# Query projections of five heads by seven products, output projections spread over the heads, and the softmax ratio on GpSimd

## The chip, the core and the metric

The kernel runs on one core of a Trainium2 chip, in one launch. The metric is the device time of that launch in microseconds (us), the median of the timed runs. Names used throughout: TensorE (PE) does matrix products, VectorE (DVE) elementwise work, ScalarE (ACT) activations and copies, GpSimd (POOL) small vector work, SyncE (SP) issues most of the DMAs.

## The reference, cut to what matters

A trunk of two layers over 16 meta tokens and 512 real ones, model width 1024, in float32: a gated linear attention layer first, then a differential attention layer with eight heads of two 128-wide maps. The change touches the second layer alone:

```python
proj = xn @ w_in                              # 1024 -> 8192
q, k, v, z = jnp.split(proj, 4, axis=-1)      # per head: q, k two maps of 128, v and z 256 wide
s = einsum(q, k) * scale + bias;  s = where(dist >= 0, s, -inf)
p = softmax(s);  a = p[:, :, 0] - lam * p[:, :, 1]
o = einsum(a, vh)
o = head_rms(o) * gnorm * (1.0 - lambda_init)
y = silu(z) * o;  h = h + y @ w_out;  out = rmsnorm(h[:, N_META:], g_final)
```

## The kernel before, in words

**Precision.** A float32 operand is split into a high part (a copy in the fast float32 format, by ACT) and a low part (source minus high part, by DVE), and a product is three passes: high by high, high by low, low by high. `split` (lines 269 to 280) does this for tokens, queries, keys and weights, so each 128x1024 piece of weights costs one ACT and one DVE instruction; its pieces are called wh and wl.

**Plain and seven-product projections.** A head needs four projections (q, k, v, z), each a 1024 by 256 piece of the weights. The plain form, `project` (line 421), takes each half of 128 output columns through 24 matmuls of 512 tokens, 48 in all. The other form, `Unit` (line 431), cuts weights and tokens into two by two blocks and forms the result by seven block products instead of eight (the scheme of Strassen and Winograd): seven products of 12 matmuls, 84 in all, each 256 or 264 tokens wide. It wants sums of token blocks (t1 to t4, made once for the layer by `token_sums2`), and for each piece of weights four additions of 128x512 blocks (line 366), three single blocks to be split (a11, a12, a22) and two pairs of blocks (s21, s43). Out of its products it makes three partial copies (u, line 452) and four additions into the result (lines 477 to 481). Before the change z, v and k of heads 1 to 7 are made by units and q of all heads by the plain form (`q_diff_q`).

**Order of the work.** PE runs in the order in which the program is written; DVE, ACT and POOL run in an order that a scheduler makes out of priorities (`urgent`, `soon`, `at_once`). A `Weaver` holds a queue of generators (projections and output projections). While head hd does its attention, `W.fill` puts pieces of that queue between the 16 attention steps: A (scores, lines 1675 to 1688), B (`turn`, transposes of the weights of attention, lines 1695 and 1696), C (`values`, lines 1400 and 1711, with the norm at 1715 to 1719) and E (`rows`, lines 1725 and 1728), over four blocks of 128 query rows, largest first. The matmuls of the scores and the values stand in a helper at line 400. The queue of a head holds z, v, k and q of the next head; the next head begins when its q is finished. In head 6, q of head 7 comes before v and z.

**Output projections.** `q_diff_out2` takes the finished rows y of two heads (two pairs of 512 output columns) and adds their product to the accumulator `hacc` (line 1771). It stands ahead of z in the queue of heads 2, 4 and 6, for the pairs (0,1), (2,3), (4,5); those of 6 and 7 are done at the end (`final_rows`).

**Homes.** The rows y of a head lie in one of two places (`yt`, by `hd % 2`). The values of a head lie in a pool with two buffers (`v_tiles`). Values leave the projection transposed, go to DRAM and come back by transposing DMAs of SP (`turn_by_dma`); `place`, `done` and `rest` then copy and split them into the value tiles, 0.0 or 11.0 us of woven work later, for odd and even heads.

**The ratio.** Behind the two exponentials of a block (line 1682), DVE takes the reciprocal of the second map's sum (line 1685), multiplies it by lambda and by the first map's sum (1686), and subtracts the maps in one instruction (1687).

**Weights.** `Weights` loads for the first two jobs of its list and prepares their pieces as soon as a buffer is free (two pairs, one of a11, a12, a22 and the sums).

## Time and profile before

| | us |
|---|---|
| timed runs (3): median, lowest, highest | 972.43, 972.37, 973.35 |
| profiled execution: span from first to last instruction | 970.2 |
| PE busy in it | 957.1 (99%) |
| DVE, ACT, POOL busy | 778.4 (80%), 628.0 (65%), 50.6 (5%) |
| heads 0 to 7 begin at (first row of each head's own woven work) | 496, 549, 601, 675, 728, 802, 854, 909 |

The page gives no total time of the profiled execution beside its span; the median of the timed runs is 2.2 us (0.23%) above the span. Busy time of PE counts a matmul from its start to a modelled end, so one matmul's busy time is longer than the step from it to the next: where a step is meant, starts are subtracted. A group's line has the source line, engine, operation and tiles, then the count, the busy time in us and the mean in ns, then the idle time of the engine ahead of it and what ended it.

### The profile page before, as it was taken

What the parts mean: (1) busy time and instruction counts of PE and PEld (TensorE: products, weight loads), DVE (VectorE), ACT (ScalarE), POOL (GpSimd) and SP (SyncE); (2) the same over time, 40 slices, a digit from 0 to 9 for tenths busy, and PEclk for the clock granted to TensorE, in tenths of its full rate; (3) what the DMA queues carried; (4) which work ended last, traced back from release to release, by engine and by line L of the source; (5) the groups of instructions that cost most, each with busy time, mean ns of one, the idle gap of its engine ahead of it and who ended that gap; (6) DMA issues with size and microseconds to landing.
All of it is one profiled execution on the core that took longest, in us unless ns stands there. A gap on an engine that the chain in (4) does not pass through costs nothing. (4 is left out here: it accounts for less than half of the span.)

```text
span 970.2 us, 18065 instructions
## 1 busy us (share of the span) xinstructions
PE 957.1 (99%) x6993; PEld 906.5 (93%) x6993; DVE 778.4 (80%) x1586; ACT 628.0 (65%) x1304; POOL 50.6 (5%) x68
## 2 busy tenths in 40 slices
PE   8999999999999999999999999999999999999997
PEld 8999999999999999898899998898998999989996
DVE  7989885886888887568997985977958879677785
ACT  7776755577647567656757774576764677655583
POOL 1000000000000100000001001001010000000001
PEclk9999999999999999999999999999999999999999
DMA  7322223635363245224355525135252352412212
GB/s 197 88 86 60 79 81 122 148 99 129 120 156 96 79 121 154 62 92 151 100 132 147 131 78 153 51 97 140 86 148 88 99 138 86 148 61 84 87 66 87
DMA packets 128521, 104.94 MB, mean 108 GB/s; under 512 B 51101, under 2 KB 112829, under 8 KB 128432
## 3 DMA queue, kind: packets, MB, share of 16 engines
q1 hardware_dynamic: 123104, 93.80, 35.1%
q10 hardware_dynamic: 5328, 9.95, 2.8%
q8 instruction: 56, 0.92, 0.4%
q14 instruction: 33, 0.27, 0.1%
HBM read 83.64 MB, written 11.80 MB: 98 GB/s over the span
## 5 line engine op out<-in xcount | busy, mean ns | idle before, releaser
L277 DVE TENSOR_TENSOR wl<-raw,wh 128x1024 fp32r<-128x1024 f32 x98 | 119.5, 1222 | 24.8 <-ACT wh L276 16.8
L276 ACT ACTIVATE wh<-raw 128x1024 fp32r<-128x1024 f32 x98 | 103.2, 1055 | 52.6 <-PE by L968 23.2
L431 PE MATMUL bv<-x,wh 128*128 128x264 f32 (+1 forms) x656 | 97.6, 286 | 0.0
L431 PE MATMUL bx<-x,wh 128*128 128x264 f32 (+1 forms) x640 | 94.9, 286 | 0.7 <-ACT u L452 0.6
L431 PEld LDWEIGHTS bv<-x,wh 128*128 128x128 f32 x656 | 86.5, 188 | 0.6 <-DVE z L479 0.3
L431 PEld LDWEIGHTS bx<-x,wh 128*128 128x128 f32 x640 | 84.5, 188 | 1.9 <-ACT u L452 1.2
L452 ACT ACTIVATE u<-bx 128x264 f32<-128x264 f32 (+1 forms) x120 | 45.4, 380 | 32.3 <-PE bx L431 31.1
L421 PE MATMUL bx<-x,wh 128*128 128x512 f32 (+1 forms) x256 | 62.4, 386 | 0.0
L277 DVE TENSOR_TENSOR wl<-sum,wh 128x1024 fp32r<-128x1024 f32 x41 | 50.1, 1221 | 14.3 <-ACT wh L276 13.9
L431 PE MATMUL bv<-x,wl 128*128 128x264 f32 (+1 forms) x328 | 55.2, 285 | 0.1
L1718 POOL TENSOR_TENSOR st<-st,mhalf 128x1 f32<-128x1 f32 x32 | 31.0, 970 | 464.4 <-ACT on L1716 408.9
L431 PE MATMUL bx<-x,wl 128*128 128x264 f32 (+1 forms) x320 | 53.9, 285 | 0.0
L1682 ACT ACTIVATE p<-p,st 128x528 f32<-128x528 f32 (+3 forms) x64 | 36.5, 571 | 25.4 <-DVE st L1680 24.9
L421 PEld LDWEIGHTS bx<-x,wh 128*128 128x128 f32 x256 | 44.5, 188 | 7.9
L276 ACT ACTIVATE wh<-sum 128x1024 fp32r<-128x1024 f32 x41 | 43.3, 1056 | 13.0 <-PE bv L431 4.0
L431 PE MATMUL by<-x,a12h 128*128 128x264 f32 (+1 forms) x320 | 46.5, 285 | 0.2 <-ACT t L1646 0.2
L431 PE MATMUL bx<-x,a11h 128*128 128x264 f32 (+1 forms) x320 | 46.3, 285 | 0.0
L431 PEld LDWEIGHTS bv<-x,wl 128*128 128x128 f32 x328 | 45.9, 188 | 0.4 <-issue 0.3
L431 PEld LDWEIGHTS bx<-x,wl 128*128 128x128 f32 x320 | 45.2, 188 | 0.6 <-DVE wl L277 0.2
L276 ACT ACTIVATE a11h<-raw 128x512 fp32r<-128x512 f32 x41 | 25.7, 627 | 28.6 <-DMA raw<-in_diff_w_in_dram 14.2
L431 PEld LDWEIGHTS bx<-x,a11h 128*128 128x128 f32 x320 | 42.2, 188 | 0.7
L431 PEld LDWEIGHTS by<-x,a12h 128*128 128x128 f32 x320 | 41.8, 188 | 0.4 <-ACT t L1646 0.4
(475 smaller groups left out, 2632.2 us busy)
## 6 DMA issues: line engine op xcount, KB each, us to landing
raw<-in_gla_w_in_dram SPq DMA_DIRECT2D x48, 512.0 KB, 4.5
raw<-in_diff_w_in_dram SPq DMA_DIRECT2D x42, 512.0 KB, 4.8
raw<-in_diff_w_in_dram SPq DMA_DIRECT2D x11, 1024.0 KB, 6.3
raw<-in_gla_w_out_dram SPq DMA_DIRECT2D x8, 1024.0 KB, 5.7
raw<-in_diff_w_out_dram SPq DMA_DIRECT2D x8, 1024.0 KB, 6.4
vd<-planes ACTq DMA_DIRECT2D x12, 268.0 KB, 7.1
vd<-keep ACTq DMA_DIRECT2D x12, 264.0 KB, 2.3
T<-bdr SPq DMA_DIRECT2D x8, 264.0 KB, 5.0
```

The lines of the kernel that those rows point to most:

```text
L276: act.activation(hi, src, AF.Copy)
L277: dve.tensor_tensor(lo, src, hi.bitcast(F32), op=ALU.subtract)
L421: pe.matmul(bank, a[:, k, :], b[k] if n0 is None else b[k][:, n0 + i * nn:n0 + (i + 1) * nn], start=n == 0 and ks[0] == 0, stop=n == len(t ...
L431: pe.matmul(bank[:, :x[q].shape[2]], w[p][:, k * P:(k + 1) * P], x[q][:, k, :], start=first and i == 0, stop=i == len(PASSES) - 1, skip_gr ...
L452: W.moved = act.activation(t, self.bx[:, :self.n], AF.Copy, scale=self.sc)
L1682: act.activation(p[:, :nk], p[:, :nk], AF.Exp, scale=-1.0, bias=st[:, m:m + 1], accum_out=st[:, 2 + m:3 + m])
L1718: pool.tensor_tensor(ms, ms, mhalf[:, :1], op=ALU.pow)
```

## The change

Four things are changed together; PE's order is the same up to head 2 of the second layer; heads 0 and 1 are touched only by the ratio and by when the values are placed.

1. **Queries of heads 3 to 7** go through a `Unit` (84 matmuls of 256 tokens) in place of the plain form (48 of 512). The unit's result lands in two float32 tiles and is split from there (`tail`).
2. **Output projections** are woven a half at a time: columns 0 to 511 of a pair in the even head, the rest in the odd head behind it; the last pair (4,5) keeps both halves in head 6. So that the rows of a pair live one head longer, rows get a third home, `y3`, and go by `hd % 3`.
3. **Values** have one home in place of two: they are placed only once their head has begun (`ready`, `begun`), 1.0 us of woven work after that. The last head's values take over `y3`.
4. **The ratio** goes to GpSimd in three instructions (power, times lambda, product); DVE keeps the subtraction of the maps.

```diff
     def turn_by_dma(planes, groups, ends, us, done, last, direct=False, ready=None):
...
-            W.follow((us, place), (1.5, lambda: done(raw[:, :, :P], tick[0], 0)), (2.5, lambda: done(raw[:, :, P:], tick[0], 1)),
+            steps = ((us, place), (1.5, lambda: done(raw[:, :, :P], tick[0], 0)), (2.5, lambda: done(raw[:, :, P:], tick[0], 1)),
                      (1.5, rest))
+            if ready is None:
+                W.follow(*steps)
+            else:
+                ready(steps)
...
     def v_tiles(s):
-        s.v = [T(ep, [P, 4, 256], F32R, f"v{i}") for i in range(2)]
+        if s is heads[-1]:
+            t = T(ep, [P, 2, 2, NR], F32R, "y3", bufs=1)
+            s.v = [t[:, j].rearrange("p a (b c) -> p (a b) c", c=256) for j in range(2)]
+        else:
+            s.v = [T(ep, [P, 4, 256], F32R, f"v{i}", bufs=1) for i in range(2)]
...
-                                      [(slice(3, 1, -1), 0), (slice(1, None, -1), 272)], 240, 0.0 if heads.index(s) % 2 else 11.0, done, last)
+                                      [(slice(3, 1, -1), 0), (slice(1, None, -1), 272)], 240, 1.0, done, last, ready=lambda steps: W.follow(*steps) if s.begun else ready.append(steps))
...
     def q_diff_q(hd, s):
+        scale, qts = -float(P) ** -0.5, []
+
+        def tiles():
+            assert not hd or heads[hd - 1].scored
+            s.q = [T(ep, [P, 2, NR], F32R, f"q{j}", bufs=1) for j in range(2)]
+
+        if hd in (3, 4, 5, 6, 7):
+            def dst():
+                tiles()
+                qts.extend([tok_tile()[:, :NR], tok_tile()[:, :NR]])
+                return qts
+
+            @soon
+            def tail(i):
+                split(*[t[:, i, :] for t in s.q], qts[i])
+
+            return W.add(Unit(want_unit(d_w_in, 256 * hd), Xr, scale, dst, tail), 8.9)
         want_diff(256 * hd)
...
-            dve.reciprocal(st[:, 5:6], st[:, 3:4])
-            dve.scalar_tensor_tensor(st[:, 5:6], st[:, 5:6], lam, st[:, 2:3], op0=ALU.mult, op1=ALU.mult)
+            pool.tensor_tensor(st[:, 5:6], st[:, 3:4], minus, op=ALU.pow)
+            pool.tensor_tensor(st[:, 4:5], st[:, 2:3], lam, op=ALU.mult)
+            pool.tensor_tensor(st[:, 5:6], st[:, 5:6], st[:, 4:5], op=ALU.mult)
             dve.scalar_tensor_tensor(r.p[0], r.p[1], st[:, 5:6], r.p[0], op0=ALU.mult, op1=ALU.subtract)
...
-    def q_diff_out2(hd, yp):
+    def q_diff_out2(hd, yp, halves):
...
-            for i in range(2):
+            for i in halves:
...
-        return W.add(gen(), 22.4)
+        return W.add(gen(), 11.2 * len(halves))
...
+    yt = [yt[:, 0], yt[:, 1], T(ep, [P, 2, 2, NR], F32R, "y3", bufs=1)]
...
         W.finish(projs[hd])
         W.settle()
-        s.scored = False
+        for chain in ready:
+            W.follow(*chain)
+        ready.clear()
+        s.scored, s.begun = False, True
...
-        if hd in (2, 4, 6):
-            out2 = q_diff_out2(hd - 2, ys[hd - 2:hd])
+        if 2 <= hd < D_HEADS - 1:
+            pair = hd - 2 - hd % 2
+            out2 = q_diff_out2(pair, ys[pair:pair + 2], range(2) if hd == D_HEADS - 2 else [hd % 2])
...
-                ys.append([yt[:, hd % 2, i] for i in range(2)])
+                ys.append([yt[hd % 3][:, i] for i in range(2)])
```

**PE at the end of a query projection.** The first rows are of the kernel before, where the queries of head 4 end (bx is the bank they gather in, x the tokens, wh and wl the weights) and the output projection of heads 0 to 3 begins (hT holds the rows y).

```order
L421 MATMUL bx_11926<-x_1514_8556,wh_11859 128x512
L421 MATMUL bx_11926<-x_1515_8557,wh_11859 128x512
L421 MATMUL bx_11926<-x_1512_8554,wl_11860 128x512 x4
L421 MATMUL bx_11926<-x_1514_8556,wl_11860 128x512 x4
L400 MATMUL bx_11960<-wh_11972,hT_8779 128x512
L400 MATMUL bx_11960<-wl_11973,hT_8779 128x512
L400 MATMUL bx_11960<-wh_11972,hT_8779 128x512 x2
```

The same place now: the last two of the seven products, 256 tokens wide, with the second half of the output projection of heads 2 and 3 behind them (y is the third home).

```order
L431 MATMUL by_12067<-x_1514_8558,a12l_11908 128x256 x4
L431 MATMUL bx_12081<-x_1544_8789,a22h_12005 128x256 x8
L431 MATMUL bx_12081<-x_1544_8789,a22l_12006 128x256 x4
L431 MATMUL bv_12028<-x_1514_8558,wh_12001 128x256
...
L431 MATMUL bv_12028<-x_1514_8558,wl_12002 128x256 x4
L400 MATMUL bx_12112<-wh_12125,y_1540_8782 128x512
L400 MATMUL bx_12112<-wl_12126,y_1540_8782 128x512
L400 MATMUL bx_12112<-wh_12125,y_1540_8782 128x512 x2
```

The first scores of a head that begins with an output projection stand, in both kernels, 18 matmuls of 512 columns behind the last query matmul. Before, that was so in heads 2, 4 and 6; now it is so in heads 2 to 6.

**DVE at the start of head 4.** Before: the low parts of the queries (line 280, the second one read straight out of PSUM) and the first scores (line 1680).

```order
L280 SCALAR_TENSOR_TENSOR q_2136_11923<-bx_11868,q_2135_11922 128x512
L1728 TENSOR_TENSOR yt_11942<-ps_11939,z_10814 128x256
L277 TENSOR_TENSOR hT_8779<-yt_11942,hT_8779 128x2x128
L277 TENSOR_TENSOR wl_11977<-raw_11964,wh_11976 128x1024
L280 SCALAR_TENSOR_TENSOR q_2136_11923<-bx_11926,q_2135_11922 128x512
L1680 ISA p_12002,st_12001<-ps_12003,T_11698 128x264
```

Now, from the addition that ends the unit (line 481) to the first scores (line 1710); `tick` opens the placing of the head's values.

```order
L481 SCALAR_TENSOR_TENSOR t_12064<-bv_12028,u_12026 128x256
L366 TENSOR_TENSOR raw_12122<-raw_12122 128x4x128
L277 TENSOR_TENSOR wl_12130<-raw_12116,wh_12129 128x1024
L277 TENSOR_TENSOR q_2161_12063<-t_12065,q_2160_12062 128x512
L277 TENSOR_TENSOR q_2161_12063<-t_12064,q_2160_12062 128x512
L616 MEMSET tick_12150 128x1
L366 TENSOR_TENSOR raw_12122<-raw_12122,sum_12140 128x4x128
L277 TENSOR_TENSOR a22l_12270<-raw_12122,a22h_12269 128x512
L1710 ISA p_12170,st_12169<-ps_12171,T_11708 128x264
```

Both halves of the queries' low parts now stand behind the unit's last addition, and so behind PE's last query matmul.

**The ratio of the first block of head 4.** Before, on DVE, from the last of the scores to the subtraction of the maps (line 1687):

```order
L1680 ISA st_12001 128x1
L366 TENSOR_TENSOR sum_12098<-raw_11980 128x512
L277 TENSOR_TENSOR a12l_12157<-raw_11980,a12h_12156 128x512
L366 TENSOR_TENSOR sum_12098<-sum_12098,raw_11980 128x512
L1685 RECIPROCAL st_12001<-st_12001 128x1
L1771 TENSOR_TENSOR keep_8187<-keep_8187,bx_11960 128x512
L1686 SCALAR_TENSOR_TENSOR st_12001<-st_12001,lam 128x1
L277 TENSOR_TENSOR wl_12036<-raw_11970,wh_12035 128x1024
L1687 SCALAR_TENSOR_TENSOR p_12002<-p_12014,st_12001,p_12002 128x528
```

Now, on DVE, over the same stretch:

```order
L1710 ISA st_12169 128x1
L412 SCALAR_TENSOR_TENSOR vm_12160<-lands_12120,short,vm_12160 32x256
L277 TENSOR_TENSOR wl_12207<-sum_12140,wh_12206 128x1024
L1718 SCALAR_TENSOR_TENSOR p_12170<-p_12182,st_12169,p_12170 128x528
L1802 TENSOR_TENSOR keep_8189<-keep_8189,bx_12112 128x512
```

Five other instructions of DVE stood between scores and subtraction, and now two; the ratio's two instructions are gone from DVE, and the subtraction there waits for GpSimd.

More of the change, by code (lines that the diff above doesn't have):

```diff
@@ L576, in landed, with turn_by_dma @@
         dve.tensor_tensor(lo, src, hi.bitcast(F32), op=ALU.subtract)
-    def turn_by_dma(planes, groups, ends, us, done, last, direct=False):
+    def turn_by_dma(planes, groups, ends, us, done, last, direct=False, ready=None):
         n = planes.shape[2]
@@ L621, in trunk @@
     dve.memset(mhalf, -0.5)
+    minus = cp.tile([P, 1], F32, name="minus")
+    dve.memset(minus, -1.0)
     warm = ps_tile()
@@ L1546, in trunk @@
     heads = [Head() for _ in range(D_HEADS)]
+    ready = []
     for s in heads:
-        s.z = None
+        s.z, s.v, s.begun = None, None, False
     RBLK = [(NR, NM)] + [(NR - P * (j + 1), P) for j in range(4)]
@@ L1580, in post @@
         def post():
+            if s.v is None:
+                v_tiles(s)
             end = L if first else 272
@@ L1587, in done @@
         def done(pt, one, m):
+            if s.v is None:
+                v_tiles(s)
             landed(s.v[0][:, :, m * P:m * P + P], s.v[1][:, :, m * P:m * P + P], pt, one)
@@ L1613, in dst @@
         def dst():
-            v_tiles(s)
             vts.extend([tok_tile(), tok_tile()])
@@ L1656, in gen @@
                 yield from project(ws.take(), real2, None, NR, [by_halves(bank)])
-                assert not hd or heads[hd - 1].scored
                 if i == 0:
-                    s.q = [T(ep, [P, 2, NR], F32R, f"q{j}", bufs=1) for j in range(2)]
-                urgent(split)(*[t[:, i, :] for t in s.q], bank, scale=-float(P) ** -0.5)
+                    tiles()
+                urgent(split)(*[t[:, i, :] for t in s.q], bank, scale=scale)
         return W.add(gen(), 10.3)
@@ L1752, in want_last @@
         return t
-    def q_diff_out2(hd, yp):
-        parts = [ws.want((d_w_out, 256 * hd, 4, 512 * i),
-                         [Part("pair", lambda raw, j=j: block_pair(raw[:, 2 * j:2 * j + 2, :])) for j in range(2)])
-                 for i in range(2)]
+    def q_diff_out2(hd, yp, halves):
+        parts = {i: ws.want((d_w_out, 256 * hd, 4, 512 * i),
+                            [Part("pair", lambda raw, j=j: block_pair(raw[:, 2 * j:2 * j + 2, :])) for j in range(2)])
+                 for i in halves}
         def gen():
-            for i in range(2):
+            for i in halves:
                 banks = [pb_tile(tag) for tag in ("bx", "by", "bv", "bx")]
```

## The prediction

> **What bounds the kernel now.** I read the page's busy times first, then PE's waits in the second layer, then a table of stretches, one for each head.
>
> ```profile
> span 970.2 us, 18065 instructions
> PE 957.1 (99%) x6993; PEld 906.5 (93%) x6993; DVE 778.4 (80%) x1586; ACT 628.0 (65%) x1304; POOL 50.6 (5%) x68
> engine line waited for: us in total, times, longest us
> PE bx L431 <- ACT u L452: 0.6, 2, 0.4
> PE ps L400 <- DVE yt L1728: 0.2, 1, 0.2
> PE by L431 <- ACT t L1646: 0.2, 1, 0.2
> ```
>
> The span is PE's own work: 13.1 us without it in 970.2, and from 480 us on only 1.0 us of named waits. So a matmul less is time less, as long as the others keep up. The table says how near they are (the first four rows are heads 2 to 5 whole, the last three the stretches of heads 3, 5 and 1 in which units run back to back):
>
> ```profile
> core 0: us, PE busy (x) PEld busy (x) DVE busy (x) ACT busy (x) POOL busy (x), PEclk, DMA share, GB/s
> 600.70:674.70 74.00, 74.00 (x484) 67.71 (x484) 59.36 (x123) 44.73 (x96) 5.94 (x4) 1.00 0.36 106
> 674.70:727.80 53.10, 52.55 (x388) 49.80 (x387) 41.05 (x97) 37.43 (x88) 5.49 (x4) 1.00 0.38 108
> 727.80:801.70 73.90, 73.90 (x483) 67.74 (x482) 61.15 (x127) 46.68 (x101) 2.95 (x4) 1.00 0.40 106
> 801.70:854.40 52.70, 52.56 (x388) 49.80 (x387) 39.71 (x92) 35.53 (x84) 2.98 (x4) 1.00 0.35 109
> 674.70:715.50 40.80, 40.24 (x329) 39.79 (x328) 34.60 (x85) 30.19 (x70) 2.60 (x2) 1.00 0.33 99
> 801.70:842.10 40.40, 40.26 (x329) 39.78 (x328) 33.19 (x80) 28.71 (x69) 1.95 (x3) 1.00 0.36 112
> 548.80:587.65 38.85, 38.85 (x322) 38.81 (x321) 32.78 (x81) 28.93 (x69) 3.34 (x2) 1.00 0.40 107
> ```
>
> The clock is granted in full. DVE is the nearest rival: 201.3 us busy in the 253.7 us of these four heads (79%), and 82 to 85% in the dense stretches, where PE stands idle 0.56, 0.14 and 0.00 us.
>
> **The queries, on PE.** The steps between starts give the price of a matmul. First the end of head 4's queries (512 tokens), then one product of 256 tokens in a unit, then the first scores of head 4:
>
> ```profile
> 725.92 2.02 PE L421 MATMUL bx<-x,wl 128*128 128x512 f32 x8
> 727.78 0.39 PE L400 MATMUL bx<-wh,hT 128*128 128x512 f32 x1
> ...
> 502.29 1.11 PE L431 MATMUL bv<-x,wh 128*128 128x256 f32 x8
> 503.23 0.65 PE L431 MATMUL bv<-x,wl 128*128 128x256 f32 x4
> 503.71 1.10 PE L431 MATMUL bx<-x,wh 128*128 128x256 f32 x8
> ...
> 731.89 0.29 PE L400 MATMUL ps<-k,q 128*128 128x264 f32 x1
> ```
>
> Eight wide ones take 727.78 - 725.92 = 1.86 us, 0.2325 each; a product of twelve takes 503.71 - 502.29 = 1.42 us, 0.1183 each. A plain query projection is 48 x 0.2325 = 11.16 us, a unit 84 x 0.1183 = 9.94. That is 1.22 us a head, **6.1 us** for five, all on the path.
>
> [...]
>
> ```profile
> L431 PEld LDWEIGHTS bv<-x,wh 128*128 128x128 f32 x656 | 86.5, 188 | 0.6 <-DVE z L479 0.3
> ```
>
> **The queries, on DVE and ACT.** Per head, from these groups (mean ns behind the busy time):
>
> ```profile
> L366 DVE TENSOR_TENSOR sum<-sum,raw 128x512 f32<-128x512 f32 x41 | 28.1, 685 | 0.3
> L277 DVE TENSOR_TENSOR a11l<-raw,a11h 128x512 fp32r<-128x512 f32 x41 | 28.1, 685 | 3.2 <-ACT a11h L276 2.0 <-PE by L431 1.1
> L479 DVE TENSOR_TENSOR t<-bv,u 128x256 f32<-128x256 f32 x7 | 2.9, 417 | 0.0
> L280 DVE SCALAR_TENSOR_TENSOR q<-bx,q 128x512 fp32r<-128x512 f32 x14 | 9.6, 684 | 0.1
> L277 DVE TENSOR_TENSOR wl<-raw,wh 128x1024 fp32r<-128x1024 f32 x98 | 119.5, 1222 | 24.8 <-ACT wh L276 16.8 <-PE bx L421 6.0 <-PE bv L431 1.4
> L276 ACT ACTIVATE a11h<-raw 128x512 fp32r<-128x512 f32 x41 | 25.7, 627 | 28.6 <-DMA raw<-in_diff_w_in_dram 14.2 <-PE bx L431 7.8 <-DMA raw<-in_gla_w_in_dram 5.1
> L452 ACT ACTIVATE u<-bx 128x256 f32<-128x256 f32 x21 | 7.9, 374 | 10.0 <-PE bx L431 10.0
> ```
>
> Two splits of 1222 ns stay (the plain halves become the pairs s21 and s43) and two splits of the result stay at about 685. New are four block additions and three single splits (7 x 0.685 = 4.80) and four additions out of PSUM (4 x 0.417 = 1.67): 6.47 us of DVE a head, 32.3 for five. ACT gets 3 x 0.627 + 3 x 0.374 = 3.0 us a head, and its 60 to 71% has room. Loads: one of 1024 KB becomes two of 512, asked for two jobs ahead, at a DMA share of 0.40 or less: nothing, covered by some 11 us of matmuls for each job.
>
> **The ratio.** DVE loses two instructions a block, the two groups below; POOL gets three, of which the first (lambda) runs during the second exponential. Neither that product nor the power of -1 stands in the trace. The nearest rows are POOL's own:
>
> ```profile
> L1685 DVE RECIPROCAL st<-st 128x1 f32<-128x1 f32 x32 | 5.0, 158 | 7.7 <-ACT p L1682 7.7
> L1686 DVE SCALAR_TENSOR_TENSOR st<-st,lam 128x1 f32<-128x1 f32 x32 | 6.9, 216 | 0.5
> L770 POOL COPY y<-t 128x64 f32<-128x64 f32 x2 | 0.5, 238 | 2.8 <-PE ps L713 1.5 <-PE by L713 1.3
> L1718 POOL TENSOR_TENSOR st<-st,mhalf x32: 550/647/3552, 518.8 to 955.6; 128x1 f32<-128x1 f32 x32
> ```
>
> So 5.0 + 6.9 = 11.9 us leave DVE. The chain of a block had 0.37 us and gets a power and a product: 0.24 + 0.55 = 0.79 us at the least, 2 x 3.55 = 7.1 at the most, and I take 2 x 0.647 = 1.3. Why the same power takes 0.55 us here and 3.55 there is in the rows of that one (667.04) and of another (792.72):
>
> ```profile
> 666.55 1.22 DVE L277 TENSOR_TENSOR wl<-raw,wh 128x1024 fp32r<-128x1024 f32 x1
> ...
> 669.50 0.69 DVE L366 TENSOR_TENSOR raw<-raw,sum 128x512 f32<-128x512 f32 x1
> 667.04 3.55 POOL L1718 TENSOR_TENSOR st<-st,mhalf 128x1 f32<-128x1 f32 x1 [7.45 <-ACT on L1716]
> ...
> 792.72 0.56 POOL L1718 TENSOR_TENSOR st<-st,mhalf 128x1 f32<-128x1 f32 x1 [6.08 <-ACT on L1716]
> 792.78 1.22 DVE L277 TENSOR_TENSOR wl<-raw,wh 128x1024 fp32r<-128x1024 f32 x1
> ```
>
> The long one ends (670.59) 0.4 us behind a run of five DVE instructions (first and last shown) that read two SBUF tiles each. The short one began 0.06 us ahead of such an instruction, and both kept their usual time: POOL waits for DVE, and DVE is not seen to wait for POOL. [...]
>
> In the new order the subtraction of the maps stands two DVE rows behind the scores where five stood, so DVE will sometimes stand at it with everything queued behind. Then it is idle, POOL has its way, and the wait is the least one: I take half a microsecond a block more than now, 16 us for 32 blocks (bounds 0 and the 1.3). That eats the 11.9 saved; for DVE the ratio is nearly neutral. For PE it is hidden between a block's scores and its transposes, 7.4 us for the first block of head 0 (500.10 + 1.64 to 509.11); without that cover it would cost up to the 1.3 - 0.37 = 0.9 us a block.
>
> ```profile
> 500.10 1.64 PE L400 MATMUL ps<-k,q 128*128 128x264 f32 x12
> ...
> 509.11 0.60 PE L1695 MATMUL ps<-ident,p 128*128 128x128 f32 x4
> ```
>
> **Halves, homes, placing.** The matmuls, loads and additions of the output projections only change heads. Spread out, they level the table above: DVE's 201.3 us get 4 x 6.47 = 25.9 for the queries and lose 16 x 0.37 = 6.0, giving 221.2 in 253.7 - 4.9 = 248.8 us, 89%, against 79%. Placing the values at the head's start moves two copies (ACT), two subtractions of 0.685 and two small ones (DVE) per head; the three transposing DMAs stay where SP issues them, long landed. The single home costs nothing: in head 3 the last value products (below) are over 6 us before the queries end at 727.78.
>
> ```profile
> 720.82 0.52 PE L400 MATMUL ps<-v,aT 128*128 128x256 f32 x3
> ```
>
> **Price of the density.** At 82 to 85% the dense stretches cost PE 0 to 0.56 us each. At 89% I take 0.4 a head, 2.0 for five (bounds 0 and 5 x 0.56 = 2.8), less the 0.7 that heads 3 and 5 lose today: **+1.3 us**.
>
> **The head's start.** Now both low parts of the queries come behind PE's last query matmul. In DVE's order stand the addition (0.42), a block addition (0.685), a wl (1.222), and the two low parts (2 x 0.685): 3.7 us, ACT's part running beside it. Ahead of the scores lie 18 matmuls, 731.89 - 727.78 = 4.1 us. That leaves 0.4 us; a DVE one wl late takes 0.8 from PE, in five heads. I take 0.2 a head, **+1.0 us** (bounds 0 and 5 x 1.22 = 6.1).
>
> **Sum:** -6.1 + 1.3 + 1.0 = -3.8 us: span 966.4, and with the 2.2 us that lie between this span and the median of the runs 968.6. The waits I priced are guesses above zero, so I put the likeliest at **968.4 us**, its own range 967 to 970.
>
> **Rivals.**
>
> *All of it arrives.* Levelling removes the idle time of heads 3 and 5 and the head's start holds: -6.1 - 0.7 = -6.8, **965.6**. For it: heads 2 and 4 have none at 80 to 83%. Against: 89%.
>
> *The head's start takes the place of the gain.* If DVE is late by one wl beyond its margin in each of five heads, 5 x 1.22 = 6.1 and the time stays at **972.4**. For it: 0.4 us of margin. Against: out of 4.1 us of cover, the chain has been paid.
>
> *DVE becomes the bound (slower).* Place: the subtraction of the maps, waiting for POOL. DVE has 248.8 - 221.2 = 27.6 us spare in 16 blocks, 1.7 us a block. If it stands w us at each, PE pays w - 1.7 over 32 blocks, and beyond w = 1.9 this outweighs 6.1. At w = 2.2 it is 16 - 6.1: **982**. For it: an exponential, a power and a product make some 2.2 us. Against: two rows of DVE work lie over that.
>
> *Narrow matmuls.* Place: the seven products, if the 188 ns of a weight load no longer hide behind a matmul half as long. At 0.133 us a step (11.16 / 84) the gain is gone; at 0.15 a unit takes 12.6, five heads lose 7.2, and with the 2.3 above it is **982**. [...] Against: the 0.1183 measured on this very form.
>
> **How the numbers follow.** Forecast 0.52, all of it 0.22, head's start 0.13, DVE 0.10, narrow 0.03. A measurement of this kernel tells a change from none at about 0.2%, 1.9 us. Below 970.5 lie the first two: 0.74. Within 970.5 to 974.4 lie most of the third: 0.13. The rest is slower: 0.13. The range takes the forecast, all of it, and the third up to no change: 965.4 to 972.4.
>
> **What would show it.** In the profile after: no 512-wide query rows beyond head 2, 256-wide steps still 0.118 us; heads 2 to 5 each some 62 us long; DVE near 89% there; POOL with 96 more instructions, none lengthening a DVE row; the scores of heads 3 to 6 within 0.5 us behind their 18 matmuls. I am wrong if PE's waits in the second layer pass 6 us, by the score rows (head's start) or by wl and a11l (density).

## The result, and the profile after

The changed kernel takes 978.72 us (median of five runs, 978.21 to 980.35) against 972.43 us; the ratio is 1.0069 with a 95% interval of 1.0058 to 1.0079. It is slower by 6.3 us, where the prediction had 968.4 and a range that ended at 972.4. The page of the kernel after begins so:

```profile
span 976.4 us, 18529 instructions
PE 956.1 (98%) x7173; PEld 912.7 (93%) x7173; DVE 796.6 (82%) x1578; ACT 638.6 (65%) x1334; POOL 83.4 (9%) x164
```

Outside PE's busy time there are now 976.4 - 956.1 = 20.3 us; there were 13.1. Named waits of PE from 480 us on come to 7.8 us, where they were 1.0. Up to the first scores of head 2 nothing is lost (they begin at 605.0 us, 604.9 before). The stretches below are heads 2 to 5 of the kernel after, each from its first scores to the next head's; the columns are those of the table in the prediction.

```profile
605.00:667.90 62.90, 62.23 (x471) 59.80 (x470) 50.03 (x104) 41.22 (x94) 7.17 (x16) 1.00 0.35 104
667.90:733.00 65.10, 63.21 (x471) 59.90 (x470) 55.32 (x114) 43.05 (x98) 8.53 (x16) 1.00 0.37 104
733.00:798.10 65.10, 63.05 (x471) 60.09 (x471) 56.25 (x116) 43.28 (x99) 7.93 (x16) 1.00 0.37 104
798.10:861.30 63.20, 62.32 (x471) 59.93 (x470) 52.73 (x109) 42.12 (x98) 7.57 (x16) 1.00 0.38 110
```

PE is idle for 0.67, 1.89, 2.05 and 0.88 us in them, 5.5 us in all. What it waits for, and what DVE and ACT wait for, the views of waits between 496 us and the tail say (PE, then DVE, then ACT):

```profile
PE bx L431 <- ACT u L452: 3.3, 4, 1.0
PE ps L400 <- DVE yt L1759: 1.2, 1, 1.2
PE ps L400 <- DVE tick L616: 1.0, 1, 1.0
PE bx L431 <- DVE keep L1802: 0.6, 1, 0.6
...
DVE p L1718 <- POOL st L1717: 27.0, 30, 2.6
...
ACT p L1712 <- DVE st L1710: 47.5, 30, 3.6
```

Line 1718 is the subtraction of the maps, 1717 GpSimd's last product, 1712 the exponential, 1710 the reduction of the scores behind which it waits, 452 the partial copy `u` of a unit. Before, the same view had this row for ACT:

```profile
ACT p L1682 <- DVE st L1680: 24.9, 17, 3.3
```

And this one in the kernel with the halves alone (H below), in which PE waits for no copy:

```profile
ACT p L1712 <- DVE st L1710: 41.8, 28, 3.6
```

Three waits hang together: DVE stands 27.0 us for GpSimd; ACT waits 47.5 us for the reductions; and PE waits four times, once in each of heads 2 to 5, for a copy that ACT makes. The sum of ACT's wait is no measure of the loss by itself, since with the halves alone it is 41.8 us and costs PE nothing: what counts is which copy it delays. One of the four, in head 4, row by row (timeline of the kernel after):

```profile
740.85 0.77 DVE L1718 SCALAR_TENSOR_TENSOR p<-p,st,p 128x528 f32<-128x528 f32 x1 [0.71 <-POOL st L1717]
...
745.01 0.64 DVE L1718 SCALAR_TENSOR_TENSOR p<-p,st,p 128x400 f32<-128x400 f32 x1 [0.61 <-POOL st L1717]
...
747.90 0.91 PE L400 MATMUL ps<-k,q 128*128 128x272 f32 x6
...
750.47 0.43 DVE L1710 CUSTOM_DVE_ANT_0 p<-ps,T 128x272 f32<-128x272 f32 x1
...
751.00 0.52 ACT L1712 ACTIVATE p<-p,st 128x272 f32<-128x272 f32 x1 [3.44 <-DVE st L1710]
...
751.52 0.36 ACT L452 ACTIVATE u<-bx 128x256 f32<-128x256 f32 x1
...
751.94 1.21 PE L431 MATMUL bx<-x,wh 128*128 128x256 f32 x8 [0.98 <-ACT u L452]
```

DVE stands at the subtractions of the first and the second block, 0.71 and 0.61 us, and its whole queue comes later. The reduction of the third block starts 750.47 - 747.90 = 2.57 us behind its scores. ACT stands 3.44 us at the exponential, and the partial copy queued behind that one starts only at 751.52 us. PE's next product into the same bank waits 0.98 us for it.

### The profile page after: what moved, and what is told of

The parts are those of the page before. It is cut to its first block, busy times and chain, and to the rows that moved or that the text cites. A ratio compares the mean times of both kernels' runs of the same rounds, so it can differ in the third digit from the quotient of the medians.

```text
span 976.4 us, 18529 instructions
## 1 busy us (share of the span) xinstructions
PE 956.1 (98%) x7173; PEld 912.7 (93%) x7173; DVE 796.6 (82%) x1578; ACT 638.6 (65%) x1334; POOL 83.4 (9%) x164
## 4 chain that ended last, share of the span: by engine, by line
PE 70%; DVE 9%; ACT 6%; issue 3%; DMA 2%; POOL 1%; POOLq 0%; SPq 0%; DVEq 0%; ACTq 0%
PE bx L431 17%; PE bv L431 10%; PE by L431 9%; PE ps L400 7%; PE bx L974 5%; PE bx L421 4%; PE by L974 2%; PE bv L974 2%; DMA raw<-in_diff_w_in_dram 2%; PE ps L1216 2%; DVE wl L277 1%; PE bx L400 1%; ACT wh L276 1%; ACT p L1712 1%; PE bx L1826 1%
## 5 line engine op out<-in xcount | busy, mean ns | idle before, releaser
L277 DVE TENSOR_TENSOR wl<-raw,wh 128x1024 fp32r<-128x1024 f32 x93 | 113.2, 1220 | 18.4 <-ACT wh L276 18.0
L431 PE MATMUL bv<-x,wh 128*128 128x264 f32 (+1 forms) x736 | 110.5, 287 | 0.3 <-DVE t L479 0.3
L431 PE MATMUL bx<-x,wh 128*128 128x264 f32 (+1 forms) x720 | 107.2, 286 | 3.4 <-ACT u L452 3.3
L431 PEld LDWEIGHTS bx<-x,wh 128*128 128x128 f32 x720 | 94.8, 188 | 5.1 <-ACT u L452 4.4
L431 PEld LDWEIGHTS bv<-x,wh 128*128 128x128 f32 x736 | 97.0, 189 | 1.3 <-DVE t L479 0.5
L431 PE MATMUL bx<-x,wl 128*128 128x264 f32 (+1 forms) x360 | 60.3, 285 | 0.1
L431 PE MATMUL bx<-x,a11h 128*128 128x264 f32 (+1 forms) x360 | 53.8, 286 | 0.6 <-DVE keep L1802 0.6
L542 POOL TENSOR_TENSOR st<-st,mhalf 128x1 f32<-128x1 f32 (+1 forms) x20 | 12.1, 604 | 386.3 <-DVE st L541 386.3
L1718 DVE SCALAR_TENSOR_TENSOR p<-p,st,p 128x528 f32<-128x528 f32 (+3 forms) x32 | 18.2, 568 | 30.2 <-POOL st L1717 28.4
L400 PE MATMUL ps<-k,q 128*128 128x264 f32 (+3 forms) x240 | 37.9, 296 | 2.9 <-DVE yt L1759 1.2
```

The source lines that it names most:

```text
L277: dve.tensor_tensor(lo, src, hi.bitcast(F32), op=ALU.subtract)
L400: pe.matmul(ps, l, r, start=first and n == 0, stop=last and n == 2, **kw)
L431: pe.matmul(bank[:, :x[q].shape[2]], w[p][:, k * P:(k + 1) * P], x[q][:, k, :], start=first and i == 0, stop=i == len(PASSES) - 1, skip_gr ...
L542: pool.tensor_tensor(dst, dst, mhalf[:np_, :dst.shape[1]], op=ALU.pow)
L1718: dve.scalar_tensor_tensor(r.p[0], r.p[1], st[:, 5:6], r.p[0], op0=ALU.mult, op1=ALU.subtract)
```

## The experiments

Three parts of the change can be undone apart: Q, the queries by seven products; R, the ratio on GpSimd; H, the halves, the three homes of the rows and the single, later placed home of the values. The edits are made to the changed kernel, and all times are medians; each ratio is to the kernel before as it ran in the same comparison (median 972.05 us for QH, RH, QR and R; 972.31 for Q, H, the unread instructions and the power more; 972.14 for the two kernels with the gate's unit first and the one with three heads; 972.17 for the last three).

| kernel | us | ratio to before, 95% interval |
|---|---|---|
| H | 970.74 | 0.9986 (0.9976 to 0.9996) |
| Q | 973.59 | 1.0017 (1.0007 to 1.0026) |
| R | 973.76 | 1.0018 (1.0009 to 1.0028) |
| QH (ratio on DVE) | 970.40 | 0.9980 (0.9969 to 0.9990) |
| RH (plain queries) | 979.37 | 1.0078 (1.0056 to 1.0100) |
| QR (no halves, no homes) | 983.33 | 1.0108 (1.0091 to 1.0125) |
| QRH (the change) | 978.72 | 1.0069 (1.0058 to 1.0079) |

The ratio on GpSimd costs 1.7 us alone (R against the kernel before), 9.7 with the queries (QR against Q), 8.6 with the halves (RH against H) and 8.3 with both.

### The ratio back on DVE (QH)

```diff
-            pool.tensor_tensor(st[:, 5:6], st[:, 3:4], minus, op=ALU.pow)
-            pool.tensor_tensor(st[:, 4:5], st[:, 2:3], lam, op=ALU.mult)
-            pool.tensor_tensor(st[:, 5:6], st[:, 5:6], st[:, 4:5], op=ALU.mult)
+            dve.reciprocal(st[:, 5:6], st[:, 3:4])
+            dve.scalar_tensor_tensor(st[:, 5:6], st[:, 5:6], lam, st[:, 2:3], op0=ALU.mult, op1=ALU.mult)
```

> The changed kernel with the ratio back on VectorE (reciprocal and one product), the queries by seven products, the halves and the homes kept. Theory A (the ratio: VectorE stands at the subtraction of the maps, 27 us in all, and what stands behind it comes late): nearly all of the loss goes and the 6.1 us of the queries show, 966 to 969. Theory B (density: the units' 6.5 us of VectorE a head are too many): 974 to 978, little changed against 978.7. Theory C (placing and levelling: the values and the output projection crowd the head's start): 974 to 978.

Measured 970.40: the ratio costs 978.72 - 970.40 = 8.3 us in the company of the other parts, and without it the kernel is a little faster than before. Theory A's direction holds, its size (966 to 969) doesn't: something of 2 us or more is lost elsewhere. Of DVE's 846 instructions from 480 us on, the ratio's left aside, some 70 stand at other places in the two kernels, so this comparison alone does not tell the waiting from the new order; the kernel without a ratio (below) does. The same place of head 4 in this kernel shows the chain in time:

```profile
745.19 0.91 PE L400 MATMUL ps<-k,q 128*128 128x272 f32 x6
...
746.02 0.43 DVE L1710 CUSTOM_DVE_ANT_0 p<-ps,T 128x272 f32<-128x272 f32 x1
...
746.49 0.52 ACT L1712 ACTIVATE p<-p,st 128x272 f32<-128x272 f32 x1 [1.65 <-DVE st L1710]
...
747.02 0.36 ACT L452 ACTIVATE u<-bx 128x256 f32<-128x256 f32 x1
...
748.08 1.10 PE L431 MATMUL bx<-x,wh 128*128 128x256 f32 x8
```

The reduction starts 0.83 us behind its scores in place of 2.57, and the copy ends 748.08 - 747.38 = 0.7 us before PE comes for it.

### Plain queries (RH)

```diff
-        if hd in (3, 4, 5, 6, 7):
+        if hd in ():
```

> The changed kernel with all queries by the plain projection, the ratio on GpSimd, the halves and the homes kept. Theory A: the waits stay and the gain of the queries is gone, 976 to 984. Theory B: the waits go, 971 to 974. Theory C: 976 to 980, since the placing stays, though the query tail at the head's start is shorter.

Measured 979.37, as A and C had it and B had not: without the queries' additional DVE work the loss is the same. PE's wait for `u` is even longer there, with DVE standing a little more:

```profile
DVE p L1718 <- POOL st L1717: 31.7, 31, 2.6
...
PE bx L431 <- ACT u L452: 5.6, 5, 1.7
```

### No halves, no homes (QR)

The output projections go back to heads 2, 4 and 6, rows get two homes, values two, and they are placed as before.

```diff
-            out2 = q_diff_out2(pair, ys[pair:pair + 2], range(2) if hd == D_HEADS - 2 else [hd % 2])
+            out2 = q_diff_out2(hd - 2, ys[hd - 2:hd], range(2))
...
-                ys.append([yt[hd % 3][:, i] for i in range(2)])
+                ys.append([yt[hd % 2][:, i] for i in range(2)])
```

> The changed kernel with whole output projections in heads 2, 4 and 6, two homes for rows and two for values, values placed as before; queries by seven products and the ratio on GpSimd kept. Theory A: 974 to 979. Theory B: heads 3 and 5 have no output projection to level the load, 979 to 985. Theory C: 966 to 970.

Measured 983.33, the slowest of the seven. C (halves, homes and placing as the culprit) falls: they help. A's 974 to 979 is missed too; B's 979 to 985 holds it, but B had already missed the run before. Part of its time is not standing but the clock: in its profile two stalls of 1.8 and 2.1 us are each followed by some 3.4 us at half the clock (0.51 from 669.40 to 672.80 us and from 881.00 to 884.50; last section), some 2 x 1.7 us more. Its other stalls lie at other places than those of the changed kernel and were not taken apart.

### The ratio alone (R)

Both edits above together.

> The kernel before with the ratio on GpSimd as the only edit. Theory A: the waits of VectorE at the subtraction appear here too and cost 4 us or more, 976 to 982. Theories B and C: VectorE is less loaded here, so it costs nothing, 971.5 to 973.5.

Measured 973.76, below A's range and 0.3 above that of B and C: alone the ratio costs 973.76 - 972.05 = 1.7 us. The remarkable thing is that DVE stands as long as in the changed kernel, and PE hardly notices:

```profile
DVE p L1715 <- POOL st L1714: 26.9, 30, 2.3
...
PE bx L431 <- ACT wh L276: 0.5, 1, 0.5
PE bx L431 <- ACT u L452: 0.4, 1, 0.4
```

So how long DVE stands does not say what PE pays. What stands behind it does.

### Queries alone (Q), halves alone (H)

> Only the queries are changed; the ratio is on DVE and the output projections and the values stay as before. Theory A (the ratio's wait at the subtraction of the maps is what costs, and it costs more the fuller DVE is): without the ratio nothing stands in the way of the 6.1 us on PE but the density, so 967 to 970. Theory D (the queries by units cost by themselves in this order, 3 us or more, whatever the ratio does; the comparison without halves and homes at 983 would then owe much to them): 973 to 978.

> Only the halves, the homes and the placing are changed; queries and ratio as before. Theory A: no matmul less and no wait more, so 970.5 to 973.5. Theory D (halves, homes and placing cost by themselves; plain queries with the ratio at 979 would then owe much to them): 975 to 979.

Q alone takes 973.59: nothing of the 6.1 us arrives, and 1.3 us are lost besides (D's range, lower end); one stall of 1.85 us with slow clock behind it (0.61 from 669.60 to 673.10 us) stands in its profile (of an execution of 975.16 us). H alone takes 970.74, as A said. Its heads 2 to 5 are the cleanest of all runs, PE busy from end to end with DVE at 77 to 80%:

```profile
604.80:667.70 62.90, 62.90 (x436) 58.67 (x435) 50.01 (x109) 41.12 (x92) 2.71 (x4) 1.00 0.35 104
667.70:730.70 63.00, 63.00 (x435) 58.69 (x434) 49.92 (x109) 41.16 (x92) 2.99 (x4) 1.00 0.36 107
```

### GpSimd's instructions run, but nobody reads them

```diff
-            pool.tensor_tensor(st[:, 5:6], st[:, 3:4], minus, op=ALU.pow)
+            dve.reciprocal(st[:, 5:6], st[:, 3:4])
+            dve.scalar_tensor_tensor(st[:, 5:6], st[:, 5:6], lam, st[:, 2:3], op0=ALU.mult, op1=ALU.mult)
+            pool.tensor_tensor(st[:, 7:8], st[:, 3:4], minus, op=ALU.pow)
             pool.tensor_tensor(st[:, 4:5], st[:, 2:3], lam, op=ALU.mult)
-            pool.tensor_tensor(st[:, 5:6], st[:, 5:6], st[:, 4:5], op=ALU.mult)
+            pool.tensor_tensor(st[:, 7:8], st[:, 7:8], st[:, 4:5], op=ALU.mult)
```

> All parts but the ratio, which VectorE computes as before; GpSimd still runs its three small instructions for each block, on the same inputs, into columns that nobody reads. The orders of TensorE and VectorE are those of the kernel with the ratio on VectorE alone (970.4). Theory A (VectorE standing for GpSimd's result is what costs): 969.5 to 972, and no wait of the subtraction for GpSimd. [...]

Measured 971.14 (ratio 0.9983, 0.9969 to 0.9997), within A's range. Theory E, that GpSimd's three instructions cost by their presence, falls: the 8.3 us of the ratio do not come back. The page of this kernel has GpSimd even busier than in the changed one (91.7 us, 83.4 there) and DVE exactly as busy as with the ratio on DVE and without these instructions (803.8 us in both); 20 rows of `wl<-sum,wh` take 1222 ns in both. GpSimd's products are the rows that differ: 193 ns each in the changed kernel, where DVE stands and waits for them, they take 322 ns here, where DVE works on (groups of the unread kernel):

```profile
PE 953.7 (98%) x7173; PEld 913.1 (94%) x7173; DVE 803.8 (83%) x1642; ACT 640.0 (66%) x1334; POOL 91.7 (9%) x164
...
L1717 POOL TENSOR_TENSOR st<-st,minus 128x1 f32<-128x1 f32 x32 | 22.6, 705 | 23.2 <-ACT p L1712 23.2
...
L1719 POOL TENSOR_TENSOR st<-st 128x1 f32<-128x1 f32 x32 | 10.3, 322 | 2.5
```

### One power more

```diff
-            pool.tensor_tensor(st[:, 5:6], st[:, 3:4], minus, op=ALU.pow)
+            pool.tensor_tensor(st[:, 7:8], st[:, 3:4], minus, op=ALU.pow)
+            pool.tensor_tensor(st[:, 5:6], st[:, 7:8], one1, op=ALU.pow)
```

> The whole change, with one power more (to the power of one) in GpSimd's chain of each block; the other engines keep their order but for four exchanged pairs on VectorE. Each block's ratio is 0.7 us later. Theory A: nothing is left to take this up in heads 1 to 6, 24 blocks, so 24 x 0.7 = 17 us of standing, of which half to all reaches TensorE: 986 to 997. Theory E (GpSimd's presence): a third more of its instructions, 980 to 983. A theory by which the chain's length is hidden and the loss is the order's: 977 to 980.

Measured 993.26 (ratio 1.0208, 1.0191 to 1.0225), within A's range: the longer chain costs 14.5 us more. Some 3 of them may be the clock, by an estimate from the mean granted clock of the two profiles (0.994 in a span of 991.3 us, 0.997 in 976.4 in the changed kernel): 991.3 x 0.006 - 976.4 x 0.003 = 3.0. One stretch of lowered clock, 0.65 from 627.20 to 630.70 us, is in the last section. DVE stands 41.7 us in place of 27.0, 14.7 more, and by the same road PE waits 7.0 us for `u`:

```profile
DVE p L1719 <- POOL st L1718: 41.7, 28, 3.3
...
PE bx L431 <- ACT u L452: 7.0, 5, 1.8
```

### The gate's unit first, with the ratio on GpSimd and on DVE

If PE pays because a partial copy of the gate's unit (z) happens to be queued behind a late exponential, then another place for the unit must help, though DVE stands as before. The half of the output projection, 11 us of PE, is queued behind the unit instead of ahead of it.

```diff
-            out2 = q_diff_out2(pair, ys[pair:pair + 2], range(2) if hd == D_HEADS - 2 else [hd % 2])
+            halves = range(2) if hd == D_HEADS - 2 else [hd % 2]
+            if hd == D_HEADS - 2:
+                out2 = q_diff_out2(pair, ys[pair:pair + 2], halves)
...
                 gates.append(q_diff_z(hd + 1, n))
+                if hd >= 2:
+                    out2 = q_diff_out2(pair, ys[pair:pair + 2], halves)
```

> The whole change, with the gate's unit of the next head queued ahead of the half of the output projection instead of behind it. In the changed kernel one stall of 0.83 to 1.14 us stands 17 to 19 us behind the start of heads 2 to 5 each, where a partial copy of the gate's unit is queued on ScalarE behind an exponential that waits for VectorE. Theory A1 (it is this meeting that TensorE pays for, a matter of place): the unit is through before that exponential, the four stalls of 3.9 us in sum go, 974 to 976. Theory A2 (what VectorE loses at the subtraction comes out somewhere, wherever the unit stands): the stalls turn up at other places, 977 to 981.

> The same move of the gate's unit, with the ratio on VectorE. Control for the run before: with the ratio on VectorE (970.4) there is no stall at that place. Both theories: 969 to 972. If the move itself costs or gains, it shows here, and is taken off the run before.

With the ratio on GpSimd it is 973.69 us, 5.0 below the changed kernel; with the ratio on DVE 970.40, no change. A2 (977 to 981) falls; A1 (974 to 976) has the direction and is 0.3 us too high. DVE stands 28.0 us, as long as ever, and ACT's wait for the reductions is down from 47.5 to 31.9 (waits of the kernel with the gate's unit first and the ratio on GpSimd):

```profile
DVE p L1718 <- POOL st L1717: 28.0, 29, 2.6
...
ACT p L1712 <- DVE st L1710: 31.9, 23, 3.7
...
PE bx L431 <- ACT u L452: 1.0, 1, 1.0
```

### Why the queries bring nothing: three heads, no ratio, four heads

The first edit has the ratio on DVE and takes the queries of heads 4 and 7 back; the second and third leave the ratio out (with and without Q), so that the subtraction waits for the exponentials alone; the fourth has the ratio on DVE, puts the gate's unit first and takes only head 7 back.

```diff
-        if hd in (3, 4, 5, 6, 7):
+        if hd in (3, 5, 6,):
```

```diff
-            pool.tensor_tensor(st[:, 5:6], st[:, 3:4], minus, op=ALU.pow)
-            pool.tensor_tensor(st[:, 4:5], st[:, 2:3], lam, op=ALU.mult)
-            pool.tensor_tensor(st[:, 5:6], st[:, 5:6], st[:, 4:5], op=ALU.mult)
-            dve.scalar_tensor_tensor(r.p[0], r.p[1], st[:, 5:6], r.p[0], op0=ALU.mult, op1=ALU.subtract)
+            dve.scalar_tensor_tensor(r.p[0], r.p[1], lam, r.p[0], op0=ALU.mult, op1=ALU.subtract)
```

> The ratio on VectorE, halves and homes as in the change, and queries by seven products in heads 3, 5 and 6 alone. Against halves alone (968.8 of span) the kernel with five such heads has its heads 2 to 6 by -0.3, +0.6, -0.1, -1.1 and +1.0 us: the queries of heads 4 and 7 lose. Theory F (each head's gain or loss stays with it, as the low parts at its own start are late or not): -0.3 - 0.1 - 1.1 = -1.5 against halves alone, 969 to 970. Theory G (a fuller VectorE comes out at any place): no gain against halves alone, 970.5 to 972.

> Queries by products, halves and homes, and the ratio left out on every engine: the subtraction takes lambda alone as its factor, so 64 small instructions and 12 us of VectorE go, with the 0.37 us of each block's chain; what is computed is not the reference's. TensorE's order is that of the kernel with the ratio on VectorE (970.4). Theory G (VectorE's load keeps the queries' gain back): a good part of the 6.1 us comes out, 965 to 968. Theory N (the gain is lost on TensorE itself, to narrow matmuls and the order): 969.5 to 971.

> Control for the run before: plain queries, halves and homes, and the ratio left out in the same way. TensorE stands for 0.7 us in all in the second layer of the kernel with the ratio (970.7), so there is next to nothing to win: 969.5 to 971 by both theories. If it gains as much as the run before, the gain there is the ratio's and not the queries'.

> Ratio on VectorE, halves and homes, the gate's unit first, queries by products in heads 3 to 6 and plain in head 7, whose start (0.91) and the block behind it (0.76) cost TensorE 1.7 us where its query gains 1.2. Theory F (a head's loss stays with it): 0.5 us less than with five, 969.5 to 970.2. Theory G (a fuller VectorE comes out at any place): 970 to 971.5, no better than halves alone.

Three heads: 971.09 (0.9986, 0.9976 to 0.9996); four heads with the gate first: 971.37 (0.9990, 0.9981 to 0.9999). Neither is better than halves alone, so F falls: a head's gain does not stay with it. Without the ratio, 971.22 with the queries and 972.46 without (intervals 0.9979 to 0.9998 and 0.9995 to 1.0014): 6.9 us less of DVE's busy time (796.9 against 803.8) bring nothing. G in its plain form, DVE's load, falls as well, and N, narrow matmuls and the order, is nearest (its 969.5 to 971 is missed by 0.2); the queries' steps (below) leave the order, which is argued and was not tested. The control is even slower than with the ratio (970.74, and above its expected range): in its new order on DVE two waits for `u` appear that halves alone did not have (1.6 us in its view of waits).

These two runs also tell the waiting from the order. From 480 us on DVE, ACT and PE of the kernel without a ratio run the instructions of the changed kernel in the changed kernel's order (a tick and three subtractions have changed places with a neighbour), and in the same way the control has the order of RH. With the same order and nothing to wait for, the changed kernel's time falls by 978.72 - 971.22 = 7.5 us and RH's by 979.37 - 972.46 = 6.9, about 1.7 of which may be the clock (0.52 from 818.20 to 821.70 us in RH's profile; last section). DVE's new order by itself costs the rest, 971.22 - 970.40 = 0.8 (not told from none by the intervals) and 972.46 - 970.74 = 1.7. GpSimd's instructions are gone too in these kernels, but run unread they cost 971.14 - 970.40 = 0.7 us, again not told from none. The place of head 4 in the kernel without a ratio:

```profile
745.77 0.91 PE L400 MATMUL ps<-k,q 128*128 128x272 f32 x6
...
746.77 0.44 DVE L1710 CUSTOM_DVE_ANT_0 p<-ps,T 128x272 f32<-128x272 f32 x1
...
747.84 0.36 ACT L452 ACTIVATE u<-bx 128x256 f32<-128x256 f32 x1
...
748.65 1.10 PE L431 MATMUL bx<-x,wh 128*128 128x256 f32 x8
```

In that order the reduction starts 1.00 us behind its scores and the copy ends 0.45 us before PE comes for it. Of the 1.57 us by which the changed kernel is later, the two stands of 0.71 and 0.61 us are 1.32.

The stalls with the queries do not follow DVE's load. Here are two starts of scores, at head 4's beginning and in head 6, first of the kernel with the ratio on DVE, then of the one without a ratio:

```profile
731.75 1.50 PE L400 MATMUL ps<-k,q 128*128 128x264 f32 x10 [0.35 <-DVE tick L616]
...
881.33 0.56 PE L400 MATMUL ps<-k,q 128*128 128x144 f32 x3 [0.75 <-DVE yt L1758]
```

```profile
732.28 0.88 PE L400 MATMUL ps<-k,q 128*128 128x264 f32 x5 [0.88 <-DVE tick L616]
...
883.18 0.56 PE L400 MATMUL ps<-k,q 128*128 128x144 f32 x3 [0.74 <-DVE yt L1756]
```

What the scores wait for at a head's beginning is not the `tick` that the row names but the second low part of the queries, queued on DVE ahead of it and, in the kernel with the ratio on DVE, behind a `wl`:

```profile
729.27 1.22 DVE L277 TENSOR_TENSOR wl<-raw,wh 128x1024 fp32r<-128x1024 f32 x1
...
730.40 1.29 DVE L277 TENSOR_TENSOR q<-t,q 128x512 fp32r<-128x512 f32 x2
```

The pair ends at 731.69, PE's scores go on at 731.75. An order of DVE with these two rows further ahead was not tried, and it stays open how much of the queries' gain it would bring.

## Why the prediction was wrong, point by point

**The bound, right.** PE's own work sets the span: PE is busy for 957.1 of 970.2 us before and 956.1 of 976.4 after, and the named waits of PE from 480 us on went from 1.0 to 7.8 us.

**The queries on PE, nearly right.** The 256-wide step is 0.118 us (median) in the kernel after, as before; the rival of narrow matmuls falls. Summed over the steps between starts from 605 to 912 us, 420 unit matmuls take 51.6 us in the kernel with the ratio on DVE, where 240 plain ones take 56.8 in halves alone: 5.2 us saved for 6.1 predicted (stalls inside the units are counted in the 51.6).

**The head's start right, the density priced by the wrong thing, the two together too small.** The terms were +1.0 and +1.3. With the halves the queries move the time from 970.74 to 970.40, by 0.3 us, which the intervals cannot tell from none; so of 5.2 us some 4.9 are given back, twice the 2.3 predicted though within the bounds (up to 6.1 and 2.8). PE's named waits from 480 us on are 3.4 us with the queries and the ratio on DVE and 0.2 with halves alone. Of the 3.4, some 1.2 stand at the queries' low parts and the unit's last addition, the head's start; the other 2.2 are single waits at other places. At head 4's start PE loses 0.35 us by the row above (1.02 in the changed kernel), through the low part one `wl` late that the prediction named as a rival at 972.4. The density was priced by DVE's share. Over heads 2 to 5 the share is 214.3 us of 256.3 in the changed kernel (84%) and 217.3 of 251.2 with the ratio on DVE (87%), below the 89% predicted: a row's time runs on into the next row's (at 745.56 one of 0.68 us is followed after 0.60), so added row times are too much. The queries add 217.3 - 197.7 = 19.6 us in four heads, 4.9 each for 6.47, and the ratio's move took 778.4 - 769.6 = 8.8 us off DVE (R) for 11.9. Nor does the price follow from the share: taking 6.9 us off DVE brought nothing.

**Halves, homes, placing: better than nothing.** They were costed at zero, less 0.7 us lost today in heads 3 and 5. Alone they give 0.14% (ratio 0.9986; 970.74 against 972.31).

**The ratio: the step that failed.** "For DVE the ratio is nearly neutral. For PE it is hidden between a block's scores and its transposes." Its parts were well sized: a power takes 0.55 us (median), a product 0.19, and DVE stands 27.0 us at 30 subtractions where 16 were taken. What it read from the rows of before, that GpSimd's run long beside DVE's work and DVE's keep their time, showed in the unread run too (GpSimd's products 322 ns against 193, DVE's `wl<-sum,wh` 1222 ns with and without them). Wrong was where the price was looked for. The ratio's own block does have its cover: no named wait of PE is for a subtraction. But behind the subtraction stand the next block's reductions, behind these, on ACT, that block's exponential (3.44 us of waiting in head 4), and behind this a partial copy that PE needs after one product of 1.42 us (0.98 us of waiting). The prediction had DVE stand "with everything queued behind" and stopped there: it did not go on to who waits for that. With DVE's order held, that waiting is 7.5 us. The prediction's own sign, more than 6 us of waits of PE in the second layer, came (7.8), but not at the rows that it named alone: 2.6 us stand at scores, none at `wl` or a11l, and the largest, 3.3, at `u`.

**The rival "DVE becomes the bound"** had the place, the subtraction waiting for GpSimd, with a chance of 0.10. Its price was wrong: it let PE pay only beyond 1.7 us of standing a block, the average spare time. DVE stands 27.0 / 30 = 0.9 us a block, and PE pays 8.3 us. Spare time elsewhere in a head is no cover for the copy that is late here. Nor is standing as such the price: 26.9 us of it cost 1.7 us in the order of before, 28.0 cost 973.69 - 970.40 = 3.3 with the gate's unit first, 27.0 cost 8.3 in the order of the change, and 14.7 more of it there cost 14.5 more (some 3 of these by the clock, as estimated above).

**Why the order of the change is the dear one.** The halves put 11 us of output projection ahead of the gate's unit in each of heads 2 to 5. Thereby the unit's second partial copy falls 17 to 19 us behind the head's start in heads 2 to 5, on the third block's exponential; the four waits for `u` in the table of the result stand at 622.21, 686.81, 751.94 and 815.67 us. Moving the unit takes 5.0 us of the 8.3 away. The remaining 3.3 were not taken apart. Nor is this the only dear order: with the queries and without the halves the ratio costs 9.7 us (983.33 - 973.59), at other waits (the longest of PE there, 2.1 us, is for a low part of the values) and with up to 3.4 us by the clock. Which meetings cost what in that order stays open.

**The sum by the runs:** halves -1.6, queries with them -0.3, ratio in their company +8.3, together +6.4 against the 6.3 measured. These are differences from kernel to kernel, so they must add up; the test of the cause is the kernel with the same order and no wait.

The versions with halves and the ratio on DVE beat both kernels, by 0.10 to 0.21% against the one before (best: the gate's unit first, five heads of queries, 0.9979, 0.9970 to 0.9989). The queries and the gate's place make no difference between them that these intervals can tell.

## What to carry to other kernels

A result fetched from another engine costs what is queued behind the instruction that waits for it: here 26.9 us of such standing cost 1.7 us in the order of before, 27.0 cost 8.3 in that of the change. Follow that queue over every engine until something has no cover left; an engine's average spare time and the waiting instruction's own cover don't tell it. And where matmuls are taken out of a stretch in which PE is the bound, the copies and splits that PE needs there come due sooner, so the saving is worth only what their place in the queues allows: here 5.2 us fewer of matmuls brought 0.3.

## What the hardware showed beside that

Behind some stalls PE's granted clock is about half for a while. In the kernel without halves and homes PE does nothing from 878.5 to 880.6 us; for the 3.5 us from 881.0 on the granted clock is 0.51 (windows; the first three columns are stretch, length and PE, and the clock is the third from the end):

```profile
877.50:878.50 1.00, 1.00 (x4) 0.38 (x2) 0.64 (x2) 0.97 (x3) 1.00 (x2) 1.00 0.00 0
878.50:880.60 2.10, 0.00 (x1) 0.00 (x0) 1.72 (x4) 0.49 (x1) 0.24 (x2) 1.00 0.84 259
880.60:881.00 0.40, 0.39 (x3) 0.39 (x4) 0.40 (x1) 0.00 (x0) 0.00 (x0) 1.00 1.08 384
881.00:884.50 3.50, 3.50 (x15) 3.21 (x15) 1.36 (x3) 0.65 (x3) 0.52 (x1) 0.51 0.29 100
```

It is not every stall. In the kernel with one power more, two waits for `u` of the same length stand at 627.15 and 762.42 us; behind the first the clock falls and 20 matmuls are done in 3.5 us, behind the second it stays and 29 are done:

```profile
627.15 0.62 PE L431 MATMUL bx<-x,wh 128*128 128x256 f32 x3 [1.79 <-ACT u L452]
...
762.42 0.74 PE L431 MATMUL bx<-x,wh 128*128 128x256 f32 x4 [1.78 <-ACT u L452]
...
627.20:630.70 3.50, 3.50 (x20) 3.50 (x21) 2.02 (x3) 1.73 (x4) 1.30 (x3) 0.65 0.12 41
762.40:765.90 3.50, 3.48 (x29) 3.48 (x30) 2.16 (x4) 1.99 (x6) 1.77 (x4) 1.00 0.33 107
```

In windows of half a microsecond the kernel with plain queries has 0.85 from 818.00 to 818.50 us, 0.50 from there to 821.50 and 0.73 up to 822.00, and 1.00 on both sides: some 3.4 us at half the clock, in which 0.5 x (0.15 + 6 x 0.50 + 0.27) = 1.7 us are lost, as much as the stall of 1.73 us ahead of it. These are the stalls whose clock the windows give, with the mean clock of the stretch behind them:

| kernel | idle of PE, us | stretch behind it | granted clock |
|---|---|---|---|
| QR | 2.11 | 881.00 to 884.50 | 0.51 |
| Q | 1.85 | 669.60 to 673.10 | 0.61 |
| QR | 1.80 | 669.40 to 672.80 | 0.51 |
| one power more | 1.79 | 627.20 to 630.70 | 0.65 |
| one power more | 1.78 | 762.40 to 765.90 | 1.00 |
| RH | 1.73 | 818.20 to 821.70 | 0.52 |
| the change | 1.22 | 887.70 to 891.20 | 1.00 |

The length of the stall alone does not tell them apart (1.78 us without, 1.73 with a slow stretch behind it), and what does was not shown.

In the changed kernel's profile no such stretch lies in the heads (1.00 in the four windows at the top), so it has no part in the explanation above. The windows show one stretch each in Q, RH and the kernel with one power more, and two in QR, each worth some 1.7 us of the profiled execution by the sum above. With one power more the mean clock of the profile is 0.994, as in QR, where Q, RH and the change have 0.997; a second stretch there would agree with it, but no window shows one.
